# A row-wise log-sum-exp: merged sums, a tapered end, and the store on another queue

## Chip, cores and metric

One NeuronCore of a Trainium2 chip. The metric is the device time of one execution in microseconds (us). "Span" is the time from the first to the last instruction in a profile; the device time is 1.8 to 2.2 us more. A load "lands" when all its data are there; the "tail" is the work left after the last landing. All runs here are of the fast state. They fell on several chips of the same kind, which differ: on some, the load stream stalls now and then. So kernels are compared within one batch of runs on one chip, each against runs of the kernel before in the same rounds.

## The reference

```python
def setup_inputs():
    batch, seq, dim = 32, 512, 1024
    return {"x": np.random.randn(batch, seq, dim).astype(np.float32), "axis": -1}

def reference(x, axis):
    x_max = np.max(x, axis=axis, keepdims=True)
    return (x_max.squeeze(axis) + np.log(np.sum(np.exp(x - x_max), axis=axis))).astype(np.float32)
```

16384 rows of 1024 floats, 67 MB in and 64 KB out. Both kernels leave the maximum out, as the values are normal random numbers.

## The kernel before

Each of the 128 partitions has 128 rows ("slices"). Thirty-one groups of four slices are loaded (2 MB each); ScalarE (ACT) takes the exponential of a whole group into bf16, and VectorE (DVE) sums each slice. The last four slices come one by one and are summed by ACT itself, through its accumulator ("fused").

```python
SLICES_PER_DMA = 4; DMA_BUFS = 9; EXP_BUFS = 5; TAIL_SLICES = 4
# ... cut
for d in range(n_body):                                  # 31 groups
    t0 = d * K
    x_tile = load(t0, K)                                 # nc.sync.dma_start, 2 MB
    exp_tile = epool.tile([P, K, D], bf16, name="exp_tile")
    nc.scalar.activation(out=exp_tile, in_=x_tile, func=exp_f, bias=0.0, scale=1.0)
    for k in range(K):
        t = t0 + k
        nc.vector.reduce_sum(out=sums[:, t : t + 1], in_=exp_tile[:, k, :],
                             axis=mybir.AxisListType.X)
for t in range(n_body * K, NT):                          # 4 fused slices
    x_tile_t = xpool.tile([P, 1, D], fp32, name="x_tile_t", bufs=4)
    nc.sync.dma_start(out=x_tile_t, in_=...)
    fused_slice(x_tile_t[:, 0, :], t)                    # activation with accum_out
nc.scalar.activation(out=res, in_=sums, func=mybir.ActivationFunctionType.Ln)
nc.sync.dma_start(out=out_view, in_=res)
```

The softmax here doesn't subtract the row's maximum and nothing guards it: scores larger than these inputs give would overflow.

## Time and profile before

| | before |
|---|---|
| time, median of the first 4 runs | 170.17 us (170.02 to 170.81) |
| span of the profiled run | 168.5 us |
| DVE busy | 142.5 us, 124 reductions |
| ACT busy | 119.2 us |
| load stream | about 428 GB/s up to about 160 us |
| last landing / DVE's last sum / logarithm's end | 160.9 / 164.2 / 165.9 us |

The lines behind this table stand in the prediction. Read it from the bottom: the stream fixes when the last byte is there, and the work that then remains fixes the end. The work at the end includes a table load: ACT needs another function table for the logarithm than for the exponential, and loading it took 1.28 us. An engine's busy share says little here, since each engine, when it is idle, waits for the stream or for the other engine.

Two more lines matter later. This is the order of time on ACT near the start of the kernel before (start, length, instruction, then idle time before it and what ended it):

```profile
13.04 3.62 ACT L100 ACTIVATE exp_tile<-x_tile 128x4096 bf16<-128x4096 f32 x1 [1.24 <-DMA x_tile<-in_x_dram]
18.70 3.62 ACT L100 ACTIVATE exp_tile<-x_tile 128x4096 bf16<-128x4096 f32 x1 [2.04 <-DMA x_tile<-in_x_dram]
```

Groups should start 4.9 us apart; here 5.66 passed. In the trace eight 16 KB packets took 1.1 to 1.5 us at that moment where 0.61 is usual. This is one of the stalls mentioned above; I overlooked it when I predicted.

### The profile page before, as it was taken

How to read it: one execution, taken by the hardware profiler on the slowest of the kernel's cores; microseconds unless marked ns; L12 is line 12 of the kernel's file. 1: busy time of each engine (PE TensorE's matmuls, PEld its weight loads, DVE VectorE, ACT ScalarE, POOL GpSimd, SP SyncE). 2: the span in 40 equal slices, each digit the busy share in tenths (PEclk: the TensorE clock that was granted, in tenths of full speed). 3: DMA queues.
4: the chain of work that ended last, by engine and by line, in shares of the span. 5: the costliest groups of instructions: out<-in, count | busy, mean ns of one | idle time of the engine just before them, and what ended most of it. 6: DMA issues, size and time to landing. Idle time of an engine off the chain costs nothing.

```text
span 168.5 us, 297 instructions
## 1 busy us (share of the span) xinstructions
DVE 142.5 (85%) x124; ACT 119.2 (71%) x42; POOL 0.2 (0%) x4
## 2 busy tenths in 40 slices
DVE  0019979989999999999999999999999999999990
ACT  3088567688766668876666787666678766667983
POOL 0000000000000000000000000000000000000000
DMA  5999999999999999999999999999999999999900
GB/s 206 420 428 397 432 428 420 424 432 436 432 432 420 416 428 428 430 424 424 432 432 428 428 432 436 424 420 428 432 428 432 428 432 424 432 420 408 382 6 16
DMA packets 5186, 67.19 MB, mean 399 GB/s; under 512 B 576, under 2 KB 704, under 8 KB 1216
## 3 DMA queue, kind: packets, MB, share of 16 engines
q1 hardware_dynamic: 5184, 67.18, 94.5%
q14 instruction: 2, 0.02, 0.0%
HBM read 67.11 MB, written 0.07 MB: 399 GB/s over the span
## 4 chain that ended last, share of the span: by engine, by line
DMA 90%; ACT 3%; DVE 2%; SPq 2%; DVEq 1%; issue 0%; ACTq 0%
DMA x_tile<-in_x_dram 90%; ACT exp_tile L100 2%; DVE sums L109 2%; SPq L56 2%; ACT L120 1%; DVEq L163 1%; ACTq L163 0%; ACTq L100 0%; ACTq L120 0%
## 5 line engine op out<-in xcount | busy, mean ns | idle before, releaser
L109 DVE TENSOR_REDUCE sums<-exp_tile 128x1 f32<-128x1024 bf16 x124 | 142.5, 1211 | 21.7 <-ACT exp_tile L100 21.7
L100 ACT ACTIVATE exp_tile<-x_tile 128x4096 bf16<-128x4096 f32 x31 | 112.1, 3617 | 45.4 <-DMA x_tile<-in_x_dram 45.4
L73 ACT ACTIVATE x_tile_t<-x_tile_t 128x1024 f32<-128x1024 f32 x4 | 4.2, 1039 | 0.0
L100 ACT ACT_TABLE_LOAD x1 | 1.3, 1283 | 0.7 <-PEq L149 0.7
L120 ACT ACT_TABLE_LOAD x1 | 1.3, 1283 | 0.6 <-DVE sums L109 0.6
L73 ACT ACTIVATION_READ_ACCUMULATOR x_tile_t<-x_tile_t 128x1 f32 x4 | 0.7, 186 | 0.0
L120 ACT ACTIVATE res<-sums 128x128 f32<-128x128 f32 x1 | 0.3, 309 | 0.0
L149 POOL MEMSET const-bfloat16-1.0<- 128x1 bf16 x1 | 0.1, 102 | 0.0
L149 POOL MEMSET const-uint8-127<- 128x1 uint8 x1 | 0.1, 102 | 0.0
L149 POOL MEMSET const-float32-0.0<- 128x1 f32 x1 | 0.1, 99 | 0.2 <-issue 0.2
L149 POOL MEMSET const-float32-1.0<- 128x1 f32 x1 | 0.1, 99 | 0.0
## 6 DMA issues: line engine op xcount, KB each, us to landing
x_tile<-in_x_dram SPq DMA_DIRECT2D x31, 2048.0 KB, 39.1
x_tile_t<-in_x_dram SPq DMA_DIRECT2D x4, 512.0 KB, 30.1
out_dram<-res SPq DMA_DIRECT2D x1, 64.0 KB, 1.6
```

The lines of the kernel that those rows point to most:

```text
L56: nc.sync.dma_start(out=x_tile, in_=x_tiled[t0 : t0 + k].rearrange("t j d -> j t d"),)
L73: nc.scalar.activation(out=x_sl, in_=x_sl, func=exp_f, bias=bias, scale=1.0, accum_out=sums[:, t : t + 1],)
L100: nc.scalar.activation(out=exp_tile, in_=x_tile, func=exp_f, bias=0.0, scale=1.0,)
L109: nc.vector.reduce_sum(out=sums[:, t : t + 1], in_=exp_tile[:, k, :], axis=mybir.AxisListType.X,)
L120: nc.scalar.activation(out=res, in_=sums, func=mybir.ActivationFunctionType.Ln,)
L149: nc = _bacc.Bacc("TRN2", target_bir_lowering=False, num_devices=1)
L163: with _tile.TileContext(nc) as tc:
```

## The change

The intent: take DVE's last sums off the end by giving the last 12 slices to ACT, let the loads taper (four pairs, four singles), sum a group with one instruction, use the freed space for a tenth buffer, and issue the store from ACT.

```diff
-DMA_BUFS = 9
+DMA_BUFS = 10
-TAIL_SLICES = 4
+TAPER_K2_BUFS = 4
+FUSED_SLICES = 4
...
-            for k in range(K):
-                t = t0 + k
-                nc.vector.reduce_sum(
-                    out=sums[:, t : t + 1],
-                    in_=exp_tile[:, k, :],
-                    axis=mybir.AxisListType.X,
-                )
+        nc.vector.reduce_sum(
+            out=sums[:, t0 : t0 + k],
+            in_=exp_tile[:, :k, :],
+            axis=mybir.AxisListType.X,
+        )
...
+    for _ in range(k2):
+        x_tile = load(t, 2)
+        for kk in range(2):
             nc.scalar.activation(
-                out=exp_tile,
-                in_=x_tile,
+                out=x_tile[:, kk, :],
+                in_=x_tile[:, kk, :],
                 func=exp_f,
                 bias=0.0,
                 scale=1.0,
+                accum_out=sums[:, t + kk : t + kk + 1],
             )
+        t += 2
+    while t < NT:
+        fused_slice(t)
+        t += 1
...
-    nc.sync.dma_start(out=out_view, in_=res)
+    nc.scalar.dma_start(out=out_view, in_=res)
```

More of the change, by code (lines that the diff above doesn't have):

```diff
@@ L7 @@
 from concourse._compat import with_exitstack
-VARIANT = "split"
 SLICES_PER_DMA = 4
-DMA_BUFS = 9
+DMA_BUFS = 10
 EXP_BUFS = 5
-TAIL_SLICES = 4
+TAPER_K2_BUFS = 4
+FUSED_SLICES = 4
 @with_exitstack
@@ L40 @@
     bf16 = mybir.dt.bfloat16
+    exp_f = mybir.ActivationFunctionType.Exp
+    K = SLICES_PER_DMA
+    fused = FUSED_SLICES
+    k2 = TAPER_K2_BUFS
+    body_slices = NT - fused - 2 * k2
+    assert body_slices % K == 0 and body_slices > 0
     xpool = ctx.enter_context(tc.tile_pool(name="xpool", bufs=DMA_BUFS))
+    epool = ctx.enter_context(tc.tile_pool(name="epool", bufs=EXP_BUFS))
     stats = ctx.enter_context(tc.tile_pool(name="stats", bufs=1))
-    if VARIANT == "split":
-        epool = ctx.enter_context(tc.tile_pool(name="epool", bufs=EXP_BUFS))
     sums = stats.tile([P, NT], fp32)
     res = stats.tile([P, NT], fp32)
-    if VARIANT == "fused":
-        negmax = stats.tile([P, NT], fp32)
-    exp_f = mybir.ActivationFunctionType.Exp
     def load(t0, k):
-        x_tile = xpool.tile([P, k, D], fp32, name=f"x_tile")
+        x_tile = xpool.tile([P, K, D], fp32, name="x_tile")
         nc.sync.dma_start(
-            out=x_tile,
+            out=x_tile[:, :k, :],
             in_=x_tiled[t0 : t0 + k].rearrange("t j d -> j t d"),
@@ L60, in load, with split_group, fused_slice @@
         return x_tile
-    def fused_slice(x_sl, t):
-        if VARIANT == "fused":
-            nc.vector.reduce_max(
-                out=negmax[:, t : t + 1],
-                in_=x_sl,
-                axis=mybir.AxisListType.X,
-                negate=True,
-            )
-            bias = negmax[:, t : t + 1]
-        else:
-            bias = 0.0
+    def split_group(t0, k):
+        x_tile = load(t0, k)
+        exp_tile = epool.tile([P, K, D], bf16, name="exp_tile")
         nc.scalar.activation(
-            out=x_sl,
-            in_=x_sl,
+            out=exp_tile[:, :k, :],
+            in_=x_tile[:, :k, :],
             func=exp_f,
-            bias=bias,
+            bias=0.0,
+            scale=1.0,
+        )
[3 more added lines that the diff above has]
+            axis=mybir.AxisListType.X,
+        )
+    def fused_slice(t):
+        x_tile = load(t, 1)
+        nc.scalar.activation(
+            out=x_tile[:, 0, :],
+            in_=x_tile[:, 0, :],
+            func=exp_f,
+            bias=0.0,
             scale=1.0,
@@ L80, in fused_slice @@
         )
-    if VARIANT == "fused":
-        K = SLICES_PER_DMA
-        assert NT % K == 0
-        for d in range(NT // K):
-            t0 = d * K
-            x_tile = load(t0, K)
-            for k in range(K):
-                fused_slice(x_tile[:, k, :], t0 + k)
-    else:
-        K = SLICES_PER_DMA
-        tail = TAIL_SLICES
-        n_body = (NT - tail) // K
-        assert n_body * K + tail == NT, "NT must split into body DMAs and tail slices"
-        for d in range(n_body):
-            t0 = d * K
-            x_tile = load(t0, K)
-            exp_tile = epool.tile([P, K, D], bf16, name="exp_tile")
+    t = 0
+    while t < body_slices:
+        split_group(t, K)
+        t += K
+    for _ in range(k2):
+        x_tile = load(t, 2)
+        for kk in range(2):
             nc.scalar.activation(
-                out=exp_tile,
-                in_=x_tile,
+                out=x_tile[:, kk, :],
+                in_=x_tile[:, kk, :],
                 func=exp_f,
@@ L105 @@
                 scale=1.0,
+                accum_out=sums[:, t + kk : t + kk + 1],
             )
-            for k in range(K):
-                t = t0 + k
-                nc.vector.reduce_sum(
-                    out=sums[:, t : t + 1],
-                    in_=exp_tile[:, k, :],
-                    axis=mybir.AxisListType.X,
-                )
-        for t in range(n_body * K, NT):
-            x_tile_t = xpool.tile([P, 1, D], fp32, name="x_tile_t", bufs=4)
-            nc.sync.dma_start(out=x_tile_t, in_=x_tiled[t : t + 1].rearrange("t j d -> j t d"))
-            fused_slice(x_tile_t[:, 0, :], t)
+        t += 2
+    while t < NT:
+        fused_slice(t)
+        t += 1
     nc.scalar.activation(
@@ L124 @@
     )
-    if VARIANT == "fused":
-        nc.vector.tensor_tensor(
-            out=res,
-            in0=res,
-            in1=negmax,
-            op=mybir.AluOpType.subtract,
-        )
-    nc.sync.dma_start(out=out_view, in_=res)
+    nc.scalar.dma_start(out=out_view, in_=res)
 _INS = ['x', 'axis']
```

## The prediction

> **What bounds the kernel now.** I read the page's busy table and slices first, then the chain that ended last, then the order of time and the stretches at the end.
>
> ```profile
> DVE 142.5 (85%) x124; ACT 119.2 (71%) x42; POOL 0.2 (0%) x4
> ...
> DMA  5999999999999999999999999999999999999900
> GB/s 206 420 428 397 432 428 420 424 432 436 432 432 420 416 428 428 430 424 424 432 432 428 428 432 436 424 420 428 432 428 432 428 432 424 432 420 408 382 6 16
> ```
>
> No compute engine is full. The DMA row is 9 from the second slice to the 38th and then 0: 67 MB arrive at about 428 GB/s until about 160 us, and the last 8 us move nothing but the result. So there are two stages: a stream that sets the pace, and a tail.
>
> ```profile
> 77.60 39.09 DMA x_tile<-in_x_dram
> ...
> 116.74 39.10 DMA x_tile<-in_x_dram
> 155.84 0.02 issue
> 155.87 0.04 ACTq L100
> 155.90 0.04 issue
> 155.95 3.62 ACT exp_tile L100
> 159.57 0.02 issue
> 159.60 1.22 DVE sums L109
> 160.82 1.12 DVEq L163
> 161.94 2.27 DVE sums L109 x2
> ...
> 164.27 1.28 ACT L120
> 165.56 0.32 ACTq L163
> ```
>
> This is the chain in order of time. Up to 155.84 it is only loads, each 39.1 us from issue to landing. A group of four slices lands every 4.89 us (ACT's last body starts are 146.15, 151.04, 155.95), and 39.1 / 4.89 = 8: a load is issued when the load eight places earlier has landed. The built program agrees: eight completion semaphores in rotation, and each load waits for the one it takes over. What follows 155.84 is the tail: one group's exponential on ACT (3.62), its four row sums on DVE (4.60), then the table load for the logarithm, the logarithm and the store.
>
> ```profile
> 159.47 1.04 ACT L73 ACTIVATE x_tile_t<-x_tile_t 128x1024 f32<-128x1024 f32 x1
> 159.60 4.60 DVE L109 TENSOR_REDUCE sums<-exp_tile 128x1 f32<-128x1024 bf16 x4 [0.31 <-ACT exp_tile L100]
> ...
> 162.59 1.04 ACT L73 ACTIVATE x_tile_t<-x_tile_t 128x1024 f32<-128x1024 f32 x1
> 163.54 0.18 ACT L73 ACTIVATION_READ_ACCUMULATOR x_tile_t<-x_tile_t 128x1 f32 x1
> 164.27 1.28 ACT L120 ACT_TABLE_LOAD   x1 [0.55 <-DVE sums L109]
> 165.57 0.31 ACT L120 ACTIVATE res<-sums 128x128 f32<-128x128 f32 x1
> 165.90 0.35 SPq L132 DMA_DIRECT2D out_dram<-res  x1
> ```
>
> The order of time at the end shows two engines working in parallel: DVE sums the last group until 164.20, and ACT does the four fused tail slices until 163.72. ACT is only 0.5 us better, so taking DVE's part away alone would win 0.5 us. The third party is the last load: the four tail loads are issued from 121.6 to 136.3 us, and the view of their tile gives
>
> ```profile
> DMA to landing us min/median/max: 24.6/30.1/35.5
> ```
>
> so the first lands at 121.6 + 35.5 = 157.1 and the last at 136.3 + 24.6 = 160.9. Compute therefore ends 3.3 us after the last byte, and that lag is what a gentler taper can win.
>
> **What the Trainium skill says.** "ScalarE: Activation LUTs", What ACT_TABLE_LOAD costs: an ACTIVATE with immediate operands is 186 ns + 0.833 ns per element, back-to-back ones overlap by about 93 ns, and a table load is 1283 ns plus a drain of about 1380. For 1024 elements that is 1039 ns, exactly the trace's; for 4096 it is 3598, the trace has 3617; the load is 1283 here too. The drain is not in this trace: ACT ended at 163.72 and the load began at 164.27, 0.06 after DVE's end; with a drain it could not have begun before 165.1. "VectorE: DVE Perf Modes", The perf-mode tier table: tensor_reduce has only the 1x mode. At the 0.96 GHz of that page's specifications 1024 elements are 1067 ns; the trace's 1211 agree, with 144 fixed. "DMA: Bandwidth & Descriptors", Specifications, puts the ceiling at 435 GB/s; this stream, at about 428, is within 2% of it. Same page, Issuing engines are not separate DMA queues: issuing from another engine saves only sequencer time; no run here shows that yet.
>
> **The change, part by part.**
>
> Buffers 9 to 10: the four separate one-slice buffers go, so the space is the same. The tenth is worth nothing: loads wait for the eighth-previous landing, not for a free buffer (ACT frees one 3.65 us after landing, before the next landing at 4.89).
>
> Body, 31 groups to 29, four reductions merged into one: now 3 x 1.130 + 1.211 = 4.60 us per group; after, 4267 + 144 = 4.41 us. DVE falls to 29 x 4.41 = 128 us, beside the stream: no gain by itself. The last reduction would end at 149.8 + 4.4 = 154.2, off the path by 8 us. That removes the group's sums from the end.
>
> Tail, from 4 fused slices to 12 (four loads of two slices, four of one). A fused slice costs ACT 1.04 us (starts 159.47, 160.51, 161.55, 162.59), the stream supplies one in 4.89 / 4 = 1.22. The last group (number 29) lands as now near 146.1, ACT works on it from 146.15 to 149.77. At that moment three slices are already on the way in or landed, so ACT starts with a backlog and works it down by 0.18 per slice. The starts are 149.67 + 1.04 n, the 0.10 being the overlap seen at 159.47 against 159.57. Landings: pairs at 148.5, 151.0, 153.4, 155.9, ACT wants them at 149.67, 151.75, 153.83, 155.91; singles at 157.1, 158.4, 159.6, 160.9 (as now, same bytes), wanted at 157.99, 159.03, 160.07, 161.11. So ACT waits nearly nowhere: under 0.1 us at the fourth pair, with a landing to start delay of 0.11 as at 155.84. The last slice starts at about 161.15, ends 162.2, and its accumulator read ends 162.3. Three of the single slices have an added wait on an earlier ACT instruction in the built program; the values are of body groups long finished, so it costs nothing.
>
> End: the load of the table needs no DVE, so it starts at 162.35 instead of 164.27, ends 163.63; the logarithm ends at 163.95 instead of 165.88. Gain 1.93 us. The store moves from SP's queue to ACT's: 0.35 us to issue and 1.6 to land as now; the handover it saves is 0.02 us (165.88 to 165.90). From the logarithm's end to the span's end there are 168.5 - 165.88 = 2.6 us, which I keep. Span 166.6; the profiled run's time was 170.25 with a span of 168.5, so 1.75 more: 168.3. Taken from the median, 170.17 - 1.93 = 168.24.
>
> The floor with a perfect ACT: last landing 160.9 + 0.1 + 1.04 + 0.1 + 1.3 + 0.3 + 2.6 = 166.3 span. So no taper on this stream gains much more than 2.2 us.
>
> **The rivals.**
> First, smaller loads end later. The tail loads land 3.8 / 3 = 1.27 us apart where a quarter group takes 1.22. If eight small loads lose 0.05 each and the four now already do, the last landing moves by 0.1 to 0.3 us. ACT's margin is 0.1 to 0.2, so at worst 0.3 us reach the end: 168.5. For it speaks the weaker 408 and 382 GB/s in the last slices; against it, the bytes per row are still 4 KB or more.
> Second, the table load does wait for ACT to drain when it stands directly behind a slice: up to 1.38 us, giving 169.6. The 0.55 us gap of today speaks against it, but it is the one spot where today's order does not show the case.
> Third, the store from ACT's queue, used for the first time at the very end, starts slower than from SP's warm queue: an estimate of 0.2 to 0.8 us, giving 168.4 to 169.0. The trace shows no ACT store to judge by.
> Fourth, buffers do bound and the stream speeds up: at 435 instead of 428 GB/s, 157 us of stream would shorten by 2.5 us, to about 165.7, over 2% faster. Eight loads always queued and a DMA share of 0.98 to 1.02 in the stretches I took speak against it.
>
> **Range and chances.** The mechanism gives 168.2 to 168.3; the rivals are nearly all on the slow side and the runs before scatter from 170.02 to 170.81. I say 168.3, range 167.7 to 169.2. Over 2% faster means below 166.8, below the floor of 166.3 + 1.75 = 168.0 unless the stream speeds up: 3%. Over 2% slower needs a loss of 3.4 us beyond everything: 1%.
>
> **What would show it.** Right: loads still 39.1 us and 4.89 us a group; DVE about 128 us busy and done by 155 us; ACT without gaps from 146 to about 162.3; table load at 162.3 to 162.4 directly behind the last accumulator read; logarithm's end near 163.95; 2.6 us after it. Wrong: idle time of ACT before the single slices (first rival), a gap before the table load (second), a store over 2 us from issue to landing (third), a shorter spacing of groups (fourth). A time of 167.7 or less would mean that I misread the stream, one above 169.2 that the end has a cost which today's trace hides.

## The result and the profile after

The changed kernel took 169.17 us (median of 11 runs, 168.0 to 170.3), the kernel before 170.62 over all its runs so far; ratio 0.9915 (95% interval 0.9891 to 0.9939). A ratio is the mean time of one kernel's fast runs over that of the other's of the same rounds, so not quite the ratio of these medians. On a quiet chip (the first batch of experiments) it was 167.95 against 169.93, ratio 0.9883. So the gain is 1.45 us on the first chip, whose stream stalls, and 1.98 us on the quiet one; 1.93 was forecast.

The page of the changed kernel's first profile, its busy times, its DMA row and its instruction queue:

```profile
DVE 128.2 (77%) x29; ACT 120.3 (72%) x56; POOL 0.2 (0%) x4
...
DMA  5999999999999999999999999999999999999940
...
q14 instruction: 1, 0.01, 0.0%
```

DVE's 128 us are those of the forecast and the stream is as full as before. The last line counts what is fetched as instructions; it becomes important below. The order of time at its end:

```profile
156.08 0.19 ACT L98 ACTIVATION_READ_ACCUMULATOR x_tile<-x_tile 128x1 f32 x1
156.29 1.06 ACT L98 ACTIVATE x_tile<-x_tile 128x1024 f32<-128x1024 f32 x1
...
161.50 1.04 ACT L82 ACTIVATE x_tile<-x_tile 128x1024 f32<-128x1024 f32 x1
162.45 0.18 ACT L82 ACTIVATION_READ_ACCUMULATOR x_tile<-x_tile 128x1 f32 x1
162.65 1.28 ACT L111 ACT_TABLE_LOAD   x1
163.95 0.31 ACT L111 ACTIVATE res<-sums 128x128 f32<-128x128 f32 x1
164.29 0.37 ACTq L116 DMA_DIRECT2D out_dram<-res  x1
```

The table load now follows the last slice directly, with no wait for DVE. The logarithm ends at 164.26 where 163.95 was forecast. The slice at 156.29 should have started at about 156.17, a pitch of 1.04 after the one before: ACT waited there, for the fourth pair, whose load landed at 156.27. From the chain that ended last (start, length):

```profile
126.81 29.46 DMA x_tile<-in_x_dram
156.27 0.02 issue
156.29 2.19 ACT x_tile L98 x4
```

### The profile page after: what moved, and what is told of

It is laid out like the page before. It is cut to its first block, busy times and chain, and to the rows that moved or that the text cites. A ratio compares the mean times of both kernels' runs of the same rounds, so it can differ in the third digit from the quotient of the medians.

```text
span 166.8 us, 223 instructions
## 1 busy us (share of the span) xinstructions
DVE 128.2 (77%) x29; ACT 120.3 (72%) x56; POOL 0.2 (0%) x4
## 2 busy tenths in 40 slices
DMA packets 5473, 67.19 MB, mean 403 GB/s; under 512 B 608, under 2 KB 736, under 8 KB 1248
## 4 chain that ended last, share of the span: by engine, by line
DMA 93%; ACT 4%; issue 1%; SPq 0%
DMA x_tile<-in_x_dram 93%; ACT x_tile L82 2%; ACT x_tile L98 1%; ACT L111 1%; ACT res L111 0%; SPq L58 0%
## 5 line engine op out<-in xcount | busy, mean ns | idle before, releaser
L74 DVE TENSOR_REDUCE sums<-exp_tile 128x4 f32<-128x4096 bf16 x29 | 128.2, 4420 | 26.3 <-ACT exp_tile L67 26.3
L67 ACT ACTIVATE exp_tile<-x_tile 128x4096 bf16<-128x4096 f32 x29 | 104.9, 3616 | 43.1 <-DMA x_tile<-in_x_dram 43.1
L98 ACT ACTIVATE x_tile<-x_tile 128x1024 f32<-128x1024 f32 x8 | 8.3, 1043 | 0.0
L82 ACT ACTIVATE x_tile<-x_tile 128x1024 f32<-128x1024 f32 x4 | 4.2, 1038 | 0.0
L98 ACT ACTIVATION_READ_ACCUMULATOR x_tile<-x_tile 128x1 f32 x8 | 1.5, 187 | 0.0
L82 ACT ACTIVATION_READ_ACCUMULATOR x_tile<-x_tile 128x1 f32 x4 | 0.7, 185 | 0.0
```

The lines of the kernel that those rows point to most:

```text
L67: nc.scalar.activation(out=exp_tile[:, :k, :], in_=x_tile[:, :k, :], func=exp_f, bias=0.0, scale=1.0,)
L74: nc.vector.reduce_sum(out=sums[:, t0 : t0 + k], in_=exp_tile[:, :k, :], axis=mybir.AxisListType.X,)
L82: nc.scalar.activation(out=x_tile[:, 0, :], in_=x_tile[:, 0, :], func=exp_f, bias=0.0, scale=1.0, accum_out=sums[:, t : t + 1],)
L98: nc.scalar.activation(out=x_tile[:, kk, :], in_=x_tile[:, kk, :], func=exp_f, bias=0.0, scale=1.0, accum_out=sums[:, t + kk : t + kk + 1],)
```

## The experiments

Twelve kernels ran, four to a batch, five rounds each: batch A on a quiet chip, B on a chip with stalls, C on another quiet chip. All results were correct.

| batch | kernel | median us | before | ratio (95%) |
|---|---|---|---|---|
| A | after_again | 167.95 | 169.93 | 0.9883 (0.9869 to 0.9896) |
| A | store_sp | 167.72 | 169.93 | 0.9870 (0.9856 to 0.9883) |
| A | coarse_loads | 170.19 | 169.93 | 1.0014 (1.0002 to 1.0027) |
| A | merged_only | 169.16 | 169.93 | 0.9954 (0.9941 to 0.9968) |
| B | before_again | 170.93 | 170.88 | 1.0010 (0.9987 to 1.0033) |
| B | pad_dve | 170.68 | 170.88 | 0.9985 (0.9969 to 1.0000) |
| B | one_table | 167.72 | 170.88 | 0.9828 (0.9787 to 0.9869) |
| B | pairs_6 | 168.75 | 170.88 | 0.9880 (0.9844 to 0.9916) |
| C | merged_b | 169.34 | 169.94 | 0.9962 (0.9950 to 0.9975) |
| C | pad_b | 169.79 | 169.94 | 0.9989 (0.9982 to 0.9995) |
| C | nine_bufs | 167.93 | 169.94 | 0.9882 (0.9869 to 0.9896) |
| C | one_table_sp | 166.59 | 169.94 | 0.9802 (0.9788 to 0.9815) |

### The changed kernel again, on a quiet chip

No edit.

> The changed kernel unedited, for the same chip and rounds as the three beside it, and for a second profile. My theory (the end is the last fused slice on ACT, which ran 3.3 us behind the last landing before and about 0.5 us behind it now): 1.4 to 1.9 us below the kernel before, ratio 0.989 to 0.992; its spread of times somewhat wider than that of before, since a late last landing now reaches the end. Rival (the wide scatter is the chip's of that day): the same spread as before.

It gained 1.98 us, a little over the expectation, and scattered by only 0.3 us (167.81 to 168.09) where the first chip gave 2.3. The wide scatter of the first runs was therefore that chip's: the kernel before also scattered more in batch B (170.33 to 172.16) than in A (169.88 to 170.05). My theory of the scatter (a late last landing now reaches the end) is not settled by this: the changed kernel still scatters more than the kernel before, 0.28 against 0.17 us here and 2.3 against 1.5 on the first chip. The order of time at the fourth pair, and at the table load:

```profile
155.49 1.06 ACT L98 ACTIVATE x_tile<-x_tile 128x1024 f32<-128x1024 f32 x1 [0.28 <-DMA x_tile<-in_x_dram]
...
161.85 1.28 ACT L111 ACT_TABLE_LOAD   x1
```

The last whole group had started at 145.36, so by the prediction's pitch the fourth pair was wanted at 145.36 + 9.76 = 155.12 (155.91 - 146.15 = 9.76 there). It started 0.37 us late, and everything behind it followed without a gap. (The load had landed at 155.47.)

### The store back on SP's queue

```diff
-    nc.scalar.dma_start(out=out_view, in_=res)
+    nc.sync.dma_start(out=out_view, in_=res)
```

> The changed kernel with the store issued from SP's queue again, as before. Theory: the move is worth nothing; within 0.15 us of the changed kernel, landing 1.6 us after its issue. Rival (the store from ACT costs or saves time at the end): 0.3 us or more apart, in the stretch between the logarithm's end and the span's end, which is 2.5 us with the store on ACT.

It was 0.23 us faster than the changed kernel in the same batch, with adjoining but hardly overlapping runs (167.65 to 167.84 against 167.81 to 168.09). The stretch from logarithm to span's end is 2.5 us in both profiles and the landing 1.6 us after issue in both. The difference lies outside the span: device time minus span is on average 2.05 us with the store on ACT, 1.86 with it on SP and 1.79 for the kernel before in this batch. So the move is worth nothing within the span and seems to cost 0.2 us after it. What takes that time the profile does not show. It also does not hold for every kernel with its store on ACT (coarse_loads: 1.79), so I leave its cause open. The traces hold one hint that I had not followed: an 8 KB instruction fetch after the span's end stands in six of the fourteen profiles, and in those runs device time minus span is 1.87 to 2.19 us; in the eight without it, 1.78 to 1.81. Among the six are kernels with either place of the store. What the fetch belongs to was not tested.

### Coarse loads for the same 12 slices

```diff
-    for _ in range(k2):
-        x_tile = load(t, 2)
-        for kk in range(2):
+    for _ in range(3):
+        x_tile = load(t, 4)
+        for kk in range(4):
...
-        t += 2
+        t += 4
```

> The last 12 slices before the four single ones' place are still summed by fused slices on ACT, but the eight of the pairs come... in words: 12 slices in three four-slice loads and then four single ones, so 16 fused slices; the taper of the pairs is gone, the singles stay. Theory: the singles still set the last landing, so ACT is held by landings only earlier and works 16 slices at 1.04 us against 1.22 of supply; the end is as with the changed kernel or up to 0.4 us earlier. Rival (the pairs are needed to smooth the landings): ACT starts the singles late, since the last four-slice load lands near 156 and its four slices take until 160.4; then the four singles end near 164.5, about 2 us later than the changed kernel.

The expectation on record describes this kernel wrongly: after 116 body slices the three loads of four bring the counter to 128, so no single slices follow. Neither of its numbers tests anything. What the kernel does measure is the taper of loads with the same 12 fused slices and DVE equally out of the way: it took 2.24 us more than the changed kernel and even 0.26 more than the kernel before. Its order of time at the end:

```profile
159.92 1.06 ACT L98 ACTIVATE x_tile<-x_tile 128x1024 f32<-128x1024 f32 x1 [0.63 <-DMA x_tile<-in_x_dram]
...
163.05 1.04 ACT L98 ACTIVATE x_tile<-x_tile 128x1024 f32<-128x1024 f32 x1
...
164.20 1.28 ACT L111 ACT_TABLE_LOAD   x1
```

ACT waits for the last 2 MB and then has four slices to do, 4 x 1.04 us, where the taper leaves one. In this kernel, taking DVE off the path is worth nothing without small last loads (the kernel before did have four).

### Merged reductions alone

```diff
-            for k in range(K):
-                t = t0 + k
-                nc.vector.reduce_sum(out=sums[:, t : t + 1], in_=exp_tile[:, k, :], ...)
+            nc.vector.reduce_sum(out=sums[:, t0 : t0 + K], in_=exp_tile, ...)
```

> The kernel before with one change: one reduction of 128x4x1024 per group in place of four. Theory: DVE's busy time falls from 142 to about 137 us, all of it beside the stream but the last group, so the time falls by 4.60 - 4.42 = 0.18 us, ratio 0.999. Rival (DVE at 85% helped to hold the stream): 1 us or more.

It gained 0.77 us, four times what I expected, and did not fit the rival either. Its order of time:

```profile
155.01 3.62 ACT L100 ACTIVATE exp_tile<-x_tile 128x4096 bf16<-128x4096 f32 x1 [1.29 <-DMA x_tile<-in_x_dram]
158.66 4.42 DVE L107 TENSOR_REDUCE sums<-exp_tile 128x4 f32<-128x4096 bf16 x1 [0.48 <-ACT exp_tile L100]
163.16 1.28 ACT L118 ACT_TABLE_LOAD   x1 [0.38 <-DVE sums L107]
```

The tail is as forecast: DVE still ends last, 4.42 us after it starts instead of 4.60, so 0.18 us. The other 0.6 us must come from a stream that ended earlier. Only the page of the first batch shows the kernel before, on the chip with stalls; no profile of it on a quiet chip was taken. Besides the stalls and the reductions the two pages differ in the instruction queue. The first line is of the kernel before, the second fence of merged reductions:

```profile
q14 instruction: 2, 0.02, 0.0%
```

```profile
q14 instruction: 1, 0.01, 0.0%
```

Fewer instructions, one fetch fewer. The fetch of 8 KB is carried by one of the DMA engines that carry the stream, and a load has landed only when its slowest engine is done. That was a theory from the pages; the next runs tested it.

### The kernel before again, and padded reductions

The kernel before was run unedited for a profile. The padded kernel is merged reductions plus instructions that do nothing useful, none in the last group:

```diff
+            if d < n_body - 1:
+                for k in range(3):
+                    nc.vector.memset(exp_tile[:, k, 0:1], 0.0)
```

> The kernel before, unedited, for a profile on the quiet chip. Merging the reductions alone won 0.77 us where I had said 0.18; the profiles show one instruction fetch of 8 KB more in the kernel before (2 packets of the instruction queue against 1), at about 71 us, on one of the 16 DMA engines that carry the stream. Theory (the fetch delays one engine, and every load lands when its slowest engine does): ratio 1.000, two packets on the instruction queue, and one spacing of body groups near 71 us that is 0.4 to 0.7 us longer than 4.89, the last group starting near 155.6 against 155.0 with merged reductions. Rival (many short reductions slow the stream all along): all spacings some 0.02 us longer. Rival (chance): the last group starts near 155.0 as well.

> Merged reductions as in the run before, plus three one-column memsets behind each reduction but the last (90 more VectorE instructions, 121 in all against 124 in the kernel before); each group of the stream leaves VectorE the room for them, and the last group has none, so nothing on the tail changes. Results stay right: they write buffers that have been read. Theory (number of instructions, through one more instruction fetch): two packets on the instruction queue and 0.4 to 0.7 us above merged reductions, so a ratio near 0.999. Rival (length or count of the reductions themselves): as fast as merged reductions, 0.995.

This batch fell on the chip with stalls. The kernel before was equal to itself (1.001) and had two fetches, but its groups showed no step near 71 us, only stalls of 0.6 and 0.8 us near 20 and 40 us. That expectation missed; the completion signals at the end of this section show why. The padded kernel also had two fetches and lost what merging had won (0.9985), but merged reductions were not in the batch. Its groups did show a step, 0.32 us (68.06 to 73.27 in place of 4.89), behind its fetch at 70.6 us. So both were repeated together.

> Merged reductions alone, once more, so that it stands on one chip with the padded kernel; the last call fell on a chip whose stream stalls now and then, the one before on a quiet chip. On a quiet chip: 0.7 to 0.8 us below the kernel before; on one with stalls perhaps less, because a load already waits for another, later engine there.

> The padded kernel beside merged reductions on one chip. Theory (the instruction fetch at about 71 us): slower than merged reductions by about 0.6 us on a quiet chip, with one landing some 0.3 to 0.9 us late right after the fetch; 0.1 to 0.2 us below the kernel before. Rival (the four short reductions themselves): the same as merged reductions within 0.1 us.

On this quiet chip they differ by 0.45 us and their intervals do not overlap; the padded kernel is 0.15 us below the kernel before, which is the 0.18 of the shorter last sum. The rival, the short reductions themselves, is out, since both kernels have merged ones. The order of time on ACT of the padded kernel, then of merged reductions without padding:

```profile
67.19 3.62 ACT L100 ACTIVATE exp_tile<-x_tile 128x4096 bf16<-128x4096 f32 x1 [1.27 <-DMA x_tile<-in_x_dram]
72.44 3.62 ACT L100 ACTIVATE exp_tile<-x_tile 128x4096 bf16<-128x4096 f32 x1 [1.63 <-DMA x_tile<-in_x_dram]
...
155.70 3.62 ACT L100 ACTIVATE exp_tile<-x_tile 128x4096 bf16<-128x4096 f32 x1 [1.29 <-DMA x_tile<-in_x_dram]
```

```profile
67.19 3.62 ACT L100 ACTIVATE exp_tile<-x_tile 128x4096 bf16<-128x4096 f32 x1 [1.28 <-DMA x_tile<-in_x_dram]
72.08 3.62 ACT L100 ACTIVATE exp_tile<-x_tile 128x4096 bf16<-128x4096 f32 x1 [1.28 <-DMA x_tile<-in_x_dram]
...
155.30 3.62 ACT L100 ACTIVATE exp_tile<-x_tile 128x4096 bf16<-128x4096 f32 x1 [1.29 <-DMA x_tile<-in_x_dram]
```

Equal to 0.01 us from 57.40 to 67.19, with the padding at work in every group, then 0.36 us apart, and 0.40 at the end. So it is not the small instructions one by one that slow the stream. The DMA view of the padded kernel between 69 and 70 us:

```profile
q1 hardware_dynamic: 27, 0.44, 107.7%
q14 instruction: 1, 0.01, 2.0%
```

The fetch falls just before the late landing; merged reductions have none there. In the trace the fetch took 0.33 us, and the data packet that starts within 0.02 us of its end took 1.27 us instead of 0.61. The three other profiles with a fetch near 71 us (before, before_again, pad_dve) have the same pair, with packets of 1.18 to 1.20 us.

Why is the step 0.36 us and not the sum, near 1 us? The trace keeps 16 completion signals for each load (no view prints them), and ACT starts after the last. In pad_b the signals of the load before the fetch came from 66.34 to 67.08 us, and those of the next load 4.89 us later, all but one: it was due at 71.37 and came at 72.33, so 0.96 us late. As the last of the 16 was due at 71.97, 0.36 us of that shows as a late landing, and it stays so for all loads behind. In both profiles of the kernel before, one signal came 1.0 us late in the same way, but still 0.16 and 0.66 us before the last one, which the stalls had made late (the 16 signals of a load spread over 0.56 to 0.66 us before the first stall and over 1.22 and 1.85 us just before the fetch): no step. In pad_dve, where a second stall had brought the spread back to 0.75 us, the delayed signal came 0.32 us behind the time at which the last was due.

### Six pairs instead of four

```diff
-TAPER_K2_BUFS = 4
+TAPER_K2_BUFS = 6
```

> The changed kernel with six pair loads instead of four (16 fused slices). The landings of the last profile put the last landing at 160.6 in that run's time and the last slice's start at 160.7, so ACT is nearly caught up already. Theory (the end hangs on the last landing): within 0.2 us of the changed kernel. Rival (the backlog of my prediction: each further fused slice wins 0.18 us until the landing binds): 0.3 us or more faster.

Its ratio, 0.988, is that of the changed kernel (0.9883 in batch A), but with a wide interval and on another chip. The profile decides: its last slice starts at 161.59, 20.28 us after its last whole group (141.31), where the changed kernel needs 15.34 (160.70 - 145.36). The difference, 4.94, is one group's 4.89 us and 0.05 more. So ACT's backlog is no longer what binds, and more taper wins nothing. In this profile too the last landing (161.37) stands close before the last slice's start.

### Nine buffers

```diff
-DMA_BUFS = 10
+DMA_BUFS = 9
```

> The changed kernel with nine load buffers instead of ten. Theory (a load waits for the landing eight places before it, never for a buffer): the same as the changed kernel, ratio 0.988 to 0.992 to before, group spacing 4.89 us. Rival (the tenth buffer lets loads be issued earlier): slower by 0.3 us or more, and waits of the issuing queue for ACT.

The same as the changed kernel (0.9882 against 0.9883), and its view of the queue's waits shows the loads waiting for landings only. The tenth buffer is worth nothing. The profile adds something: here the four pairs land 2.49 us apart in the trace, and the fourth starts 9.89 us after the last whole group (155.34 - 145.45), against 10.13 (155.49 - 145.36) in batch A's profile of the changed kernel. There the second pair came 2.74 us after the first, right behind the instruction fetch at 149 to 150 us; the other three 2.48 to 2.49. But this kernel has a fetch there too, at 149.43, and no late landing. Of the six profiles with four pairs all have one fetch between 148.8 and 150.1; the second pair landed 0.23 to 0.34 us late in four of them, 0.11 in one, and on time in this one.

### One table set, and the best kernel

```diff
+    nc.scalar.preload_act_table_set("natural_log_exp_and_others")
```

The second kernel also has the store on SP's queue.

> The changed kernel with one table set that holds both exponential and logarithm, loaded once at the start. Theory (the end is serial: last landing, one slice, table load, logarithm, store): the 1.28 us load at the end goes and with it the 0.2 us wait around it: 1.3 to 1.5 us below the changed kernel, ratio to before near 0.980. Rival (the load is partly hidden, or the store or the closing waits end the kernel anyway): less than 0.8 us. The accuracy may differ a little, since the set is another.

> The candidate for the best: the changed kernel with one table set loaded at the start and the store from SP's queue. The single-table kernel measured 0.983 of before on the chip with stalls; the store from SP was 0.2 us faster than from ACT on the quiet chip, all of it outside the span. Theory: 1.5 to 1.8 us below the changed kernel, ratio to before 0.978 to 0.982. Rival (the 0.2 us was chance): 0.983.

The best kernel took 166.59 us, ratio 0.9802, 1.34 us below the kernel of its batch that is equal to the changed one (nine_bufs, 167.93). The expectation of 1.5 to 1.8 was too high; the ratio lies at its edge. Whether it is 2% faster than the kernel before stays unclear, as the interval contains 0.98. One table alone measured 0.983 on the chip with stalls, 1.03 us below pairs_6 of that batch; the changed kernel itself was not in it, so that run alone does not decide between its theory and its rival. The order of time at the end of the best kernel:

```profile
160.58 1.04 ACT L82 ACTIVATE x_tile<-x_tile 128x1024 f32<-128x1024 f32 x1
161.53 0.18 ACT L82 ACTIVATION_READ_ACCUMULATOR x_tile<-x_tile 128x1 f32 x1
161.74 0.31 ACT L113 ACTIVATE res<-sums 128x128 f32<-128x128 f32 x1
162.08 0.35 SPq L118 DMA_DIRECT2D out_dram<-res  x1
```

The logarithm follows the accumulator read after 0.03 us; the 1.28 us load is gone from the end and the rest of the chain is unmoved. Of the 1.34 us that is 1.28, and the store's place gives at most the rest (device time minus span is 1.84 here against 1.96 for nine_bufs). Both kernels are correct against the reference.

## Why the prediction was right, point by point

The time lay at the edge of the range, 169.17 on a chip with stalls, and the gain on quiet chips, 1.98 and 2.01 us, is the forecast 1.93. But two of its terms were wrong and cancelled each other: that the total came within 0.1 us on quiet chips was luck.

- **What bounds.** Right. The stream is unchanged at 4.89 us a group, and the gain that was forecast lies behind the last landing: coarse_loads and pairs_6 show both sides of it. The rest of the gain, about 0.6 us on the first quiet chip, does not.
- **Buffers.** Right: nine_bufs equals the changed kernel. (ACT frees a buffer 3.73 us after landing, 155.84 to 159.57, not 3.65; still before the next landing.)
- **Merged reductions, "no gain by itself" but for the 0.18 of the last group.** The durations were right (4.42 measured, 4.41 forecast, 128.2 us busy). The step that failed is the assumption that DVE's instructions cost the stream nothing. Their number caused a further instruction fetch, on the stream's own engines: 0.45 us in C (merged_b against pad_b), where the trace shows it, and by inference about 0.6 us in batch A (0.77 - 0.18), where the kernel before was not profiled. The larger loss there would fit its chip: the signals of a load spread over only 0.53 us in merged_only, so one that is 0.96 us late puts off the landing by 0.43 us at least (an estimate).
- **Tail, "ACT waits nearly nowhere".** The pitch of 1.04 us held for all 12 slices. The landings of the pairs were mis-sized: 2.49 us apart, not 4.89 / 2 = 2.45, and in most profiles one of them later still at a fetch. Over the six profiles with four pairs the fourth pair started 0.11 to 0.46 us late, and the last load landed 15.01 to 15.36 us after the last whole group, where the prediction kept the 14.84 of the kernel before although it put more and smaller loads in between. This is the first rival, which I had put at 0.3 us at worst. In all six the last slice starts about 0.15 us after the last landing, and the fourth pair could start 0.02 us after its own; so a fourth pair in time would have won 0.13 us at most (an estimate from these numbers). Between the profiles of merged_only and after_again the logarithm's end moved from 164.76 to 163.45, so 1.31 us where 1.93 - 0.18 = 1.75 was forecast; of the missing 0.44, 0.15 is a stream that started later (first group at 8.29 against 8.15 us, last whole group of after_again at 145.36 against 145.21), which is scatter. The other 0.29 is the late fourth pair, 0.37, less 0.08 that the prediction had allowed too much behind it.
- **Table load behind a slice (second rival).** No drain: 0.02 us after the accumulator read. Right.
- **Store (third rival).** Nothing within the span, about 0.2 us outside it, unexplained; it lands 1.6 us after its issue, as forecast.
- **Faster stream (fourth rival).** Not by buffers. But the stream did end earlier, by a cause that I had not on the list.
- **The sum on quiet chips.** 0.8 for the merge and 1.2 for the rest, against 0.18 and 1.75. On the first chip, with stalls, the total is 0.5 us smaller. In both profiles with stalls of the kernel before, the fetch near 71 us makes no step, because other engines are later still; in such an execution the merge cannot win its 0.6. But merged reductions were not run on such a chip, and on the other one (batch B) pairs_6, which behaves like the changed kernel, gained about 2.05 us by its ratio (1.4 to 2.7 by the interval). So the smaller total is not explained for sure.

## What to carry to other kernels

In a stream-bound kernel the end is worth reading by itself: last landing, last piece of work, table load, logarithm, store stand in series, and only what stands there counts. Small last loads shorten it until the last landing binds; after that a switch of tables (1.28 us here) is the next to go. And count instructions: a load lands with its slowest DMA engine, so one more instruction fetch in mid-stream can delay everything behind it (0.36 us here), unless another engine is later still, as it was in both profiles of the kernel before.

## What the Trainium skill lacked or had wrong

- "ScalarE: Activation LUTs", What ACT_TABLE_LOAD costs: a drain of about 1380 ns for every switch does not appear here. The load starts 0.02 us after the last accumulator read, and the next ACTIVATE 0.02 us after the load: 1.32 us from the read's end to the logarithm's start, and 1.34 us were won by leaving it out (with the store moved). The advice of the same page, Rules for kernel authors, to use the set with both functions was right.
- The same page does not give the cost of reading out the accumulator: an instruction of 185 ns, of which about half is hidden. Fused slices of 1024 elements start 1.04 us apart with it; as ACT starts an instruction about 0.09 us before the one before ends, 1039 ns alone would give 0.95 (an estimate), so it adds about 0.09 us a slice.
- "DMA: Bandwidth & Descriptors", Queues, rings and completion order: it says that row 14 is the runtime's own, but not what traffic on it costs a full stream. "Runtime: NRT & Kernel Launch", Instruction fetch mechanics, calls the cost of a fetch "mostly hidden", and does not give it either. Here an 8 KB instruction fetch made one landing 0.36 us late, and the kernel 0.45 us slower.
- The same page, Anatomy of one DMA, fits about 2 us fixed cost per DMA for another issuing path. Loads queued behind each other pay far less here: 1 MB loads land 2.49 us apart and 512 KB loads 1.28, where their shares of a 2 MB load would be 2.45 and 1.22, so 0.04 to 0.06 us a load.
- No page has the stalls that some chips showed: up to eight packets at a time took 1.0 to 2.0 us instead of 0.61, and a group landed up to 1.1 us late, once or twice in an execution.
